# A hybrid attention and convolution layer: the convolution of tiles 1 to 4 in two column blocks ahead of attention, output weights loaded behind the last k projection, four output tiles beside the last attention chunks

## The chip, the cores and the metric

The kernel runs on one core of a Trainium2 chip. The metric is the time of one execution on the device in microseconds (us); what is compared is the median of several runs. A profiled execution is one more run, recorded by the hardware; its rows give the busy time of each engine: PE (TensorE), DVE (VectorE), ACT (ScalarE), POOL (GpSimd) and SP, whose queue issues the DMA transfers. "PEld" is TensorE's weight load. The "clock" of a stretch is the TensorE clock granted in it, where 1.00 is 2.4 GHz and 0.50 is 1.2 GHz.

## What is computed

One layer over 2048 prompt frames and 8 x 16 sample frames, all in float32, model width 1024 (17 tiles of 128 frames: tile 0 holds the sample frames, tiles 1 to 16 the prompt):

```python
def layer(x, p_i, k_cache, v_cache, conv_cache, prm, i):
    hn = rmsnorm(x, prm['norm_mix'][i])
    proj = hn @ prm['w_in'][i]
    q, k, v, a, g = jnp.split(proj, SPLITS, axis=-1)
    ...
    attn = swa_prompt(q, k, v, sinks)          # or swa_sample for the sample frames
    ...
    u = a * jax.nn.sigmoid(g)
    c, new_conv = depthwise_causal(u, prm['conv_w'][i], prm['conv_b'][i], conv_cache)
    c = jax.nn.silu(layernorm(c, prm['ln_g'][i], prm['ln_b'][i]))
    merged = jnp.concatenate([rmsnorm(attn, prm['attn_out_g'][i]), rmsnorm(c, prm['conv_out_g'][i])], axis=-1)
    x = x + merged @ prm['w_out'][i]
    hf = rmsnorm(x, prm['norm_ffn'][i])
    x = x + jnp.square(jax.nn.relu(hf @ prm['w_up'][i])) @ prm['w_down'][i]
    gate = jax.nn.sigmoid(rmsnorm(x, prm['norm_ple'][i]) @ prm['w_ple_gate'][i])
    x = x + (p_i @ prm['w_ple'][i]) * gate
```

Attention runs in chunks of 64 frames over a window of 128 earlier frames (8 query heads, 2 key heads, width 64, with sinks). The convolution is depthwise over 512 channels with 31 taps.

## The kernel before

**Arithmetic.** Every large product is made of float32 operands split into a high and a low part, so that one product is three matmuls (high by high, high by low, low by high). `weight()` brings one row block of a weight in: a load into `raw` (three buffers), a cast on ACT into the high half of `w` and a subtraction on POOL (or DVE) for the low half. `wpool` has eight `w` buffers.

**Stages.** They follow each other on TensorE.
- **A** (L286 to L328): six blocks of up to three tiles. Norm, transposition and split into `hn`, which is stored to `H` in memory, then the projections a and g and their product into `U0` to `U3` (prompt, 512 frames each) and `US` (sample).
- **B** (L457 to L525): eight blocks of two tiles (the first has tile 0 too). Each loads its part of `H` back into eight `hnb` buffers, computes the projections k, v and then the four of q from six weight blocks `wq`, and runs four chunks of attention: scores `s`, a softmax on DVE and ACT (`pr`), transpositions `pt`, copies `p`, the product with v (`o`), copies into `mta`, a store to `M[t]`. One sample batch goes with each block.
- **C** (L536 to L585): for a tile, load `M[t]` and `x`, split `M[t]`, 48 matmuls with the eight weight blocks `wo` of `w_out`, residual, `X1[t]` stored, and the sum of its squares for the next norm. One tile (tile 1, `EARLY`) stands inside stage B's pools; the other eight follow.
- **MLP** (L690 to L745): five blocks of up to four tiles, 4096 hidden columns in eight groups, weights streamed. Tiles 9 to 16 have their output projection (`c_late`) between the groups of blocks 0 and 1. Then the gated embedding.

**The convolution** is cut into steps (`conv_steps`): in each, column blocks 0 to 2 are done by DVE, three multiply-adds into PSUM (L207), and column block 3 (`PCB`) by ACT, which scales a `tap`, and POOL, which adds it (L199, L200). A block of tiles takes 31 steps and one more for each tile (`conv_post`: norm, activation, transposition, store to `M[t]`). The generator `conv_a` goes through tile 0, tiles 1 to 4 and tiles 5 to 8; `A_STEPS` says how many steps follow each of a block's four column blocks in stage A, `B_STEPS` how many follow each chunk in B. Of the 102 steps of `conv_a` A takes 52 and B 50. Tiles 9 to 16 are stepped in the MLP.

**The order of the work.** A scheduler lays out one in-order queue for each engine from priorities that follow the program's text; `later` shifts the priority of what it wraps (by `BEHIND` for convolution steps, by `-PREO` for `load_wo`, by `-PRE` for `wq`), and `issue_after` keeps what it wraps behind a given instruction on that instruction's queue. Inside a queue nothing overtakes.

Of the kernel before, what the change touches and what calls it, by code (L numbers as in the profile page):

```python
# [39 lines left out]
CONV_A = [[0], [1, 2, 3, 4], [5, 6, 7, 8]]  # L40
A_STEPS = {1: 4, 2: 4, 3: 2, 4: 2, 5: 1}
B_STEPS = (2, 2)
CONV_LATE = {0: [9, 10, 11, 12], 1: [13, 14, 15, 16]}
# [8 lines left out]
EARLY = 1  # L52
# [5 lines left out]
PCB = (3,)  # L58
# [17 lines left out]
def build(ctx, tc, nc, a):  # L76
# [97 lines left out]
    def conv_steps(tiles):  # L174
# [15 lines left out]
        own = [(cb, j) for cb in range(4) if cb not in PCB for j in range(KC)]  # L190
        per = len(own) // KC
        for j in range(KC):
            for cb in PCB:
# [29 lines left out]
    conv_a = (x for tiles in CONV_A for x in conv_steps(tiles))  # L223
# [233 lines left out]
    for bi, tiles in enumerate(B_BLOCKS):  # L457
# [156 lines left out]
    def c_late_half(t, h, xt, ms):  # L614
# [8 lines left out]
        for nh in range(2):  # L623
            xs = xt[:, nh * 512:(nh + 1) * 512]
            nc.vector.scalar_tensor_tensor(xs, pd[nh], ors[:, t, h:h + 1], xs, ALU.mult, ALU.add)

    def c_late(tiles):

        load_wo()
        for i in range(0, len(tiles), 2):  # L630
            pair = [(t, *c_late_front(t)) for t in tiles[i:i + 2]]
            for h in range(2):
                for t, xt, ms in pair:
                    c_late_half(t, h, xt, ms)
            for t, xt, ms in pair:
                nc.sync.dma_start(X1[t], xt)
                ss = fpool.tile([P, 2], F32, name="osl", bufs=2)
                for nh in range(2):
                    sq = fpool.tile([P, 512], F32, name="sqx", tag="relu", bufs=2)
                    nc.scalar.activation(sq, xt[:, nh * 512:(nh + 1) * 512], AF.Square, accum_out=ss[:, nh:nh + 1])  # L640
                nc.gpsimd.tensor_tensor(ss[:, 0:1], ss[:, 0:1], ss[:, 1:2], ALU.add)
# [225 lines left out]
```

## Time and profile before

| | |
|---|---|
| median of three runs | 2563.26 us (2559.66 to 2565.75) |
| profiled execution | 2565.52 us, span 2563.7 us |
| mean granted TensorE clock | 0.986 |
| busy, share of the span | PE 98%, DVE 44%, ACT 41%, POOL 42% |

The span goes from the first to the last instruction; 1.8 us of the execution lie outside it. A busy share is an average over stages: PE is full through the MLP and gives way only at a few places, and what those places wait for has to be read one by one. A matmul's end is modelled, so that a PE that is busy at a clock of 0.50 does half of what it would at 1.00.

### The profile page before, as it was taken

The page shows a single profiled execution, that of the slowest core. Times are in us where ns is not written, and L with a number is a line of the kernel's source. Part 1 is how long each engine was busy: PE and PEld are TensorE (multiplying, and loading weights), DVE is VectorE, ACT ScalarE, POOL GpSimd, SP SyncE. Part 2 cuts the span into 40 slices and gives each one's busy share as a digit, 9 for nine tenths or more (in the row PEclk, how much of TensorE's full clock was granted, in tenths as well). Part 3 has the DMA queues.
Part 4 walks back from the last instruction along what each step waited for, and adds up shares of the span by engine and source line. Part 5 has one row for each costly group of instructions (what it writes and reads, how often), then busy time and mean ns, then how long its engine had stood idle before and what let it go on. Part 6 is the DMA issues. An engine that isn't in the chain of part 4 may idle for free.

```text
span 2563.7 us, 32974 instructions
## 1 busy us (share of the span) xinstructions
PE 2503.8 (98%) x12575; PEld 2120.4 (83%) x12575; DVE 1115.8 (44%) x1874; ACT 1060.9 (41%) x2027; POOL 1084.7 (42%) x783
## 2 busy tenths in 40 slices
PE   8998999997999999999999999999999999999998
PEld 8998877665888888888888888888899998998887
DVE  3654647663355543455535242222322234344433
ACT  6362467675232223633233332323233334454343
POOL 5062034036264444855343543435355555642222
PEclk9998999997999999999999999999999999999999
DMA  8434222222452232523234552323344336553221
GB/s 242 152 121 147 78 96 71 83 81 91 155 197 100 95 111 90 206 83 115 83 115 148 184 199 81 115 74 120 120 163 132 131 124 208 186 189 115 91 72 49
DMA packets 121998, 321.39 MB, mean 125 GB/s; under 512 B 15728, under 2 KB 49264, under 8 KB 121840
## 3 DMA queue, kind: packets, MB, share of 16 engines
q1 hardware_dynamic: 121840, 319.29, 37.1%
q8 instruction: 98, 1.61, 0.3%
q14 instruction: 60, 0.49, 0.1%
HBM read 264.95 MB, written 54.29 MB: 125 GB/s over the span
## 4 chain that ended last, share of the span: by engine, by line
PE 94%; ACT 2%; DMA 2%; DVE 1%; POOL 1%; issue 1%; SPq 0%; POOLq 0%; ACTq 0%; DVEq 0%
PE up L273 29%; PE d L729 29%; PE mm L273 12%; PE pg L751 7%; PE acc L546 4%; PE accl L620 3%; PE o L404 2%; PE pq L758 2%; PE s L376 1%; DMA hnb<-H 1%; PE pt L398 1%; PE tr L661 1%; PE tr L261 1%; PE pt L392 0%; PE up L261 0%
## 5 line engine op out<-in xcount | busy, mean ns | idle before, releaser
L121 POOL TENSOR_TENSOR w<-raw,w 128x1024 fp32r<-128x1024 f32 x305 | 731.5, 2412 | 708.5 <-ACT w L120 707.2
L273 PE MATMUL up<-hf,w 128*128 128x512 f32 (+2 forms) x3840 | 761.5, 357 | 0.5 <-DVE ht L715 0.5
L729 PE MATMUL d<-w,ht 128*128 128x512 f32 x3264 | 759.7, 390 | 0.3 <-ACT ht L713 0.3
L273 PEld LDWEIGHTS up<-hf,w 128*128 128x128 f32 x3840 | 659.4, 189 | 93.2 <-DVE ht L715 1.3
L729 PEld LDWEIGHTS d<-w,ht 128*128 128x128 f32 x3264 | 609.8, 188 | 125.7 <-ACT ht L713 0.8
L120 ACT CAST w<-raw 128x1024 fp32r<-128x1024 f32 x330 | 345.9, 1050 | 651.0 <-PE d L729 457.2
L735 DVE TENSOR_TENSOR accf<-d,accf 128x512 f32<-128x512 f32 x272 | 176.1, 686 | 386.7 <-PE d L729 386.1
L207 DVE SCALAR_TENSOR_TENSOR c<-U,vec,c 128x512 f32<-128x512 f32 x348 | 261.3, 751 | 6.1
L714 DVE SCALAR_TENSOR_TENSOR up<-up,relu 128x512 f32<-128x512 f32 (+2 forms) x160 | 98.9, 618 | 311.9 <-ACT relu L712 311.7
L273 PE MATMUL mm<-hn,w 128*128 128x384 f32 (+1 forms) x1152 | 200.1, 331 | 0.9 <-ACT hn L263 0.8
L273 PE MATMUL mm<-hnb,w 128*128 128x256 f32 (+1 forms) x1152 | 180.8, 307 | 15.2 <-DMA hnb<-H 11.9
L273 PEld LDWEIGHTS mm<-hn,w 128*128 128x128 f32 x1152 | 190.5, 190 | 1.7 <-ACT hn L263 1.7
L200 POOL TENSOR_TENSOR acc<-acc,tap 128x512 f32<-128x512 f32 (+1 forms) x150 | 169.3, 1129 | 44.5 <-ACT tap L199 33.9
L712 ACT ACTIVATE relu<-up 128x512 f32<-128x512 f32 (+2 forms) x160 | 84.9, 531 | 244.5 <-PE up L273 244.0
L273 PEld LDWEIGHTS mm<-hnb,w 128*128 128x128 f32 x1152 | 158.1, 196 | 32.6 <-issue 23.7
L715 DVE TENSOR_TENSOR ht<-up,ht 128x512 fp32r<-128x512 f32 (+2 forms) x160 | 97.7, 611 | 109.8 <-ACT ht L713 105.8
L751 PE MATMUL pg<-w,xg 128*128 128x512 f32 x510 | 125.2, 392 | 0.0
L751 PEld LDWEIGHTS pg<-w,xg 128*128 128x128 f32 x510 | 94.7, 188 | 18.8
L199 ACT ACTIVATE tap<-U,vec 128x512 f32<-128x512 f32 x120 | 85.0, 722 | 30.6 <-POOL acc L200 29.8
L454 POOL TENSOR_TENSOR ors<-ors,mhalf 128x1 f32<-128x1 f32 x17 | 10.5, 616 | 196.3 <-DVE ors L453 196.2
L546 PE MATMUL acc<-w,ms 128*128 128x512 f32 x384 | 91.3, 397 | 1.2 <-ACT ms L120 1.2
L713 ACT ACTIVATE ht<-relu 128x512 fp32r<-128x512 f32 (+2 forms) x160 | 90.6, 566 | 1.3
(182 smaller groups left out, 2203.1 us busy)
## 6 DMA issues: line engine op xcount, KB each, us to landing
raw<-in_w_up SPq DMA_DIRECT2D x160, 512.0 KB, 3.5
raw<-in_w_down SPq DMA_DIRECT2D x160, 512.0 KB, 3.5
H<-hn SPq DMA_DIRECT2D x20, 768.0 KB, 4.9
hnb<-H SPq DMA_DIRECT2D x56, 256.0 KB, 4.2
xt<-in_x SPq DMA_DIRECT2D x17, 512.0 KB, 6.1
xnf<-X SPq DMA_DIRECT2D x17, 512.0 KB, 5.7
accf<-X SPq DMA_DIRECT2D x17, 512.0 KB, 5.1
X<-accf SPq DMA_DIRECT2D x17, 512.0 KB, 3.2
```

The lines of the kernel that those rows point to most:

```text
L120: nc.scalar.copy(hi, src)
L121: (eng or nc.gpsimd).tensor_tensor(lo, src, hi.bitcast(F32), ALU.subtract)
L200: nc.gpsimd.tensor_tensor(acc, acc, t, ALU.add)
L207: nc.vector.scalar_tensor_tensor(accs[cb] if i == KC - 1 else pacc, view(cb, i), w_, pacc, ALU.mult, ALU.add)
L273: nc.tensor.matmul(ps, w(wp, k), m[:, ap_, 0:n], start=(i == 0), stop=(i == 3 * KD - 1))
L546: nc.tensor.matmul(ps, ms[:, ap_, k, :], wo[k][:, wp, nh * 512:(nh + 1) * 512], start=(i == 0), stop=(i == 11))
L713: nc.scalar.activation(ht[:, 0, 0:n], r[:, 0:n], AF.Square)
L714: nc.vector.scalar_tensor_tensor(ps[:, 0:n], ps[:, 0:n], 0.0, r[:, 0:n], ALU.max, ALU.mult)
L715: hs = nc.vector.tensor_tensor(ht[:, 1, 0:n], ps[:, 0:n], ht[:, 0, 0:n].bitcast(F32), ALU.subtract)
L729: nc.tensor.matmul(pd[nh], hts[f][:, hp, i * P:(i + 1) * P], wds[f][:, wp, nh * 512:(nh + 1) * 512], start=(j == 0), stop=(j == 3 * GRP - 1))
L735: ad = nc.vector.tensor_tensor(xs, pd[nh], xs, ALU.add)
L751: nc.tensor.matmul(pg, xg[ap_][:, k * P:(k + 1) * P], wg[k][:, wp, ns], start=(i == 0), stop=(i == 3 * KD - 1))
```

## The change

- `conv_steps` takes the column blocks of ACT and POOL for each block of tiles: tiles 1 to 4 give them blocks 2 and 3, and DVE two multiply-adds a step in place of three. The other blocks of tiles stay.
- `A_STEPS` puts 64 steps into A in place of 52, `B_STEPS` 38 into B in place of 50: the 31 steps of tiles 1 to 4 now all stand in A.
- Tiles 1 to 4 (`EARLY`) have their output projection inside stage B's pools, on buffers that are done there: the split in quarters of 256 columns in `hnb`'s eight buffers, `M[t]` in `US`'s, x and sum in `U0`'s and `U1`'s.
- In stage C and there the split of `M[t]` goes in four quarters, and the sum of squares on ACT is taken of each half, into the PSUM tile, and added on POOL. `c_late` does the same.
- `load_wo` is wrapped in `issue_after` with the last block's k projection.
- The convolution of tiles 9 to 16 is one generator over both MLP blocks.

```diff
-CONV_A = [[0], [1, 2, 3, 4], [5, 6, 7, 8]]
-A_STEPS = {1: 4, 2: 4, 3: 2, 4: 2, 5: 1}
-B_STEPS = (2, 2)
-CONV_LATE = {0: [9, 10, 11, 12], 1: [13, 14, 15, 16]}
+CONV_A = [([0], (3,)), ([1, 2, 3, 4], (2, 3)), ([5, 6, 7, 8], (3,))]
+CONV_LATE = [([9, 10, 11, 12], (3,)), ([13, 14, 15, 16], (3,))]
+A_STEPS = {1: 4, 2: 4, 3: 3, 4: 3, 5: 2}
+B_STEPS = (1, 2)
...
-EARLY = 1
+EARLY = 4
...
-PCB = (3,)
...
-    def conv_steps(tiles):
+    def conv_steps(tiles, pcb):
...
-    with later(tc, -PREO):
+    with later(tc, -PREO), tc.issue_after(kproj.ins):
         load_wo()
 
-    def c_tile(t, pl, ps_, mt, xt, ms, acct):
+    def residual(t, nh, xt, acc, h, ss):
+
+        xs = xt[:, nh * 512:(nh + 1) * 512]
+        nc.vector.scalar_tensor_tensor(xs, acc, ors[:, t, h:h + 1], xs, ALU.mult, ALU.add)
+        if h:
+            nc.scalar.activation(acc, xs, AF.Square, accum_out=ss[:, nh:nh + 1])
+
+    def c_end(t, xt, ss):
+        nc.sync.dma_start(X1[t], xt)
+        nc.gpsimd.tensor_tensor(ss[:, 0:1], ss[:, 0:1], ss[:, 1:2], ALU.add)
+        rstd(rs1[:, t:t + 1], ss[:, 0:1], 1.0 / D)
+
+    def c_tile(t, ps_, mt, xt, ms, acct):
+
         nc.sync.dma_start(mt, M[t])
         nc.sync.dma_start(xt, a["x"][t])
-        split(ms[:, 0], ms[:, 1], mt)
+        for i, m in enumerate(ms):
+            split(m[:, 0], m[:, 1], mt[:, 2 * i:2 * i + 2])
+        ss = cpool.tile([P, 2], F32, name="oss")
...
-                xs = xt[:, nh * 512:(nh + 1) * 512]
-                nc.vector.scalar_tensor_tensor(xs, ps, ors[:, t, h:h + 1], xs, ALU.mult, ALU.add)
-        nc.sync.dma_start(X1[t], xt)
-        ss = pl.tile([P, 1], F32, name="oss", bufs=2)
-        nc.scalar.activation(mt.rearrange("p k n -> p (k n)"), xt, AF.Square, accum_out=ss)
-        rstd(rs1[:, t:t + 1], ss, 1.0 / D)
-
-    for t in F_BLOCKS[0][:EARLY]:
-        mx_ = upool.tile([P, 2, D], F32, name="mxe", tag="U1", bufs=1)
-        c_tile(t, bpool, psb, mx_[:, 0].rearrange("p (k n) -> p k n", k=8), mx_[:, 1],
-               upool.tile([P, 2, 8, P], F32R, name="mse", tag="U0", bufs=1),
+                residual(t, nh, xt, ps, h, ss)
+        c_end(t, xt, ss)
+
+    xe = [upool.tile([P, 2, D], F32, name="xe", tag=f"U{i}", bufs=1) for i in range(2)]
+    for i, t in enumerate(F_BLOCKS[0][:EARLY]):
+        c_tile(t, psb, upool.tile([P, 8, P], F32, name="mte", tag="US", bufs=1), xe[i // 2][:, i % 2],
+               [bpool.tile([P, 2, 2, P], F32R, name="mse", tag="hnb", bufs=8, align_bytes=ALN) for _ in range(4)],
                dict(tag="mm"))
```

Lines of the changed kernel stand one lower than before from `conv_steps` on (L199 for L200), a few higher from the k projection on, and L564 for L546.

**SP's queue between A and B.** The last stores of `hn`, the last loads of `w_in` for `wq`, loads of `w_out`, and the first block's loads of `H`. Before:

```order
L294 DMA H<-hn 128x4x256 x4
L128 DMA raw<-in_w_in 128x1024 x3
L128 DMA raw<-in_w_out 128x1024 x4
L462 DMA hnb<-H 128x2x384 x8
L416 DMA vc<-in_cache_vt 128x128
L418 DMA ks<-in_cache_kt 128x128
L416 DMA vc<-in_cache_vt 128x128
L418 DMA ks<-in_cache_kt 128x128
L513 DMA out_new_conv_prompt<-U_141 512x1x30
L128 DMA raw<-in_w_out 128x1024
```

Now:

```order
L295 DMA H<-hn 128x4x256 x4
L127 DMA raw<-in_w_in 128x1024 x3
L127 DMA raw<-in_w_out 128x1024
L463 DMA hnb<-H 128x2x384 x8
L417 DMA vc<-in_cache_vt 128x128
L419 DMA ks<-in_cache_kt 128x128
L417 DMA vc<-in_cache_vt 128x128
L419 DMA ks<-in_cache_kt 128x128
L516 DMA out_new_conv_prompt<-U_141 512x1x30
L127 DMA raw<-in_w_out 128x1024 x4
```

Of the four loads of `w_out` that stood ahead of the first block's `hnb` one still does. The other three moved behind these loads, with a fifth that stood there before. None of the five moved to the last block's k projection: `load_wo` has no instruction on TensorE's queue, which is the one that `issue_after` orders here. The last three loads of `w_out` stand behind the last block's `hnb`, before and now.

**POOL's queue between A and B.** `w` by L121 (now L120) is the low half of a `wq` block; `acc` by L200 (L199) is a tap of the convolution. Before:

```order
L200 TENSOR_TENSOR acc_1454<-acc_1454,tap_3089 128x512
L200 TENSOR_TENSOR acc_1454<-acc_1454,tap_3095 128x512
L200 TENSOR_TENSOR acc_1454<-acc_1454,tap_3147 128x512
L326 COPY U3_141<-U2_140 128x4x30
L121 TENSOR_TENSOR w_2328<-raw_2326,w_2328 128x1024
L121 TENSOR_TENSOR w_2333<-raw_2331,w_2333 128x1024
L121 TENSOR_TENSOR w_2338<-raw_2336,w_2338 128x1024
L121 TENSOR_TENSOR w_2343<-raw_2341,w_2343 128x1024
L121 TENSOR_TENSOR w_2348<-raw_2346,w_2348 128x1024
L121 TENSOR_TENSOR w_2353<-raw_2351,w_2353 128x1024
L456 MEMSET qb_2318 128x1024
```

Now:

```order
L199 TENSOR_TENSOR acc_1453<-acc_1453,tap_2095 128x512
L199 TENSOR_TENSOR acc_1454<-acc_1454,tap_2098 128x512
L120 TENSOR_TENSOR w_2483<-raw_2481,w_2483 128x1024
L120 TENSOR_TENSOR w_2488<-raw_2486,w_2488 128x1024
L120 TENSOR_TENSOR w_2493<-raw_2491,w_2493 128x1024
L199 TENSOR_TENSOR acc_1453<-acc_1453,tap_2223 128x512
L199 TENSOR_TENSOR acc_1454<-acc_1454,tap_2226 128x512
L120 TENSOR_TENSOR w_2498<-raw_2496,w_2498 128x1024
L120 TENSOR_TENSOR w_2503<-raw_2501,w_2503 128x1024
L199 TENSOR_TENSOR acc_1453<-acc_1453,tap_2231 128x512
L199 TENSOR_TENSOR acc_1454<-acc_1454,tap_2234 128x512
L120 TENSOR_TENSOR w_2508<-raw_2506,w_2508 128x1024
```

Ahead of the fourth of the six `wq` blocks 48 taps of tiles 1 to 4 stand now, in two chains (`acc_1453` and `acc_1454`), where 30 stood; two stand between the third and the fourth, two between the fifth and the sixth, and ten follow.

**TensorE's queue at the end of B.** `o` is the product with v of one chunk, `s` scores, `pr` a softmax's result that is transposed into `pt`. Before (L546, one output tile, ends some 20 such lines further up, behind the last q projection):

```order
L152 MATMUL c<-ident,acc 128x128 x4
L435 MATMUL o<-vc,p_5805 128x128
L436 MATMUL o<-vn,p_5805 128x128
L440 MATMUL pt<-ident,on 128x128
L376 MATMUL s<-kt,qt 128x192 x4
L452 MATMUL pt<-ones,sra 128x1
L392 MATMUL pt<-ident,pr 128x128 x4
L398 MATMUL pt<-ident,pr 64x128 x4
L404 MATMUL o<-p_5859,va 128x512
L392 MATMUL pt<-ident,pr 128x128 x4
L169 MATMUL c<-ident,z 128x128 x4
L404 MATMUL o<-p_5866,va 128x512
```

Now (L564 is the output projection of tiles 1 to 4):

```order
L168 MATMUL c<-ident,z 128x128 x4
L377 MATMUL s<-kt,qt 128x192 x2
L441 MATMUL pt<-ident,on 128x128
L377 MATMUL s<-kt,qt 128x192 x2
L564 MATMUL acc<-w,mse 128x512 x24
L453 MATMUL pt<-ones,sra 128x1
L393 MATMUL pt<-ident,pr 128x128 x4
L564 MATMUL acc<-w,mse 128x512 x12
L399 MATMUL pt<-ident,pr 64x128 x4
L405 MATMUL o<-p_5918,va 128x512
L393 MATMUL pt<-ident,pr 128x128 x4
L405 MATMUL o<-p_5925,va 128x512
```

The 192 matmuls of four tiles stand between the last q projection and the last row shown with L564, spread among attention of the seventh block's chunks and parts of `conv_post`. Behind it six chunks follow up to stage C with nothing between them, as before. Stage C then has five tiles in place of eight.

**ACT's queue at the end of B,** up to the first split of stage C. Before:

```order
L199 ACTIVATE tap<-U_140,vec 128x512 x2
L394 COPY p_6347<-pt 128x512
L199 ACTIVATE tap<-U_140,vec 128x512
L408 COPY mta<-o 64x4x64 x2
L199 ACTIVATE tap<-U_140,vec 128x512
L199 ACTIVATE tap<-U_141,vec 128x512
L408 COPY mta<-o 64x4x64 x2
L199 ACTIVATE tap<-U_141,vec 128x512
L448 ACTIVATE pt<-mta 128x512
L448 ACTIVATE pt<-mts 128x512
L120 CAST ms<-mt 128x1024 x2
```

Now:

```order
L443 COPY mts<-pt 64x4x16 x2
L198 ACTIVATE tap<-U_141,vec 128x512 x2
L386 ACTIVATE pr<-pr,rc 128x192
L395 COPY p_6360<-pt 128x512
L395 COPY p_6406<-pt 128x512
L409 COPY mta<-o 64x4x64 x4
L449 ACTIVATE pt<-mta 128x512
L449 ACTIVATE pt<-mts 128x512
L119 CAST ms<-mt 128x256 x8
```

From the copy that stands for the product `o<-p_5866` (now `p_5925`) to the first split `ms`, 27 taps of tiles 9 to 12 and 13 to 16 stood in ACT's queue and 18 stand now.

## Rows read from the trace of the kernel before

**Rows 1.** The page: busy time of PE, and the chain that ended last by engine.

```profile
PE 2503.8 (98%) x12575; PEld 2120.4 (83%) x12575; DVE 1115.8 (44%) x1874; ACT 1060.9 (41%) x2027; POOL 1084.7 (42%) x783
...
PE 94%; ACT 2%; DMA 2%; DVE 1%; POOL 1%; issue 1%; SPq 0%; POOLq 0%; ACTq 0%; DVEq 0%
```

**Rows 2.** Busy time by stretch: PE, PEld, DVE, ACT, POOL, PE's clock, DMA share, GB/s.

```profile
205.00:232.00 27.00, 17.17 (x140) 17.00 (x140) 18.74 (x27) 9.60 (x12) 15.12 (x7) 0.84 0.64 212
260.00:532.00 272.00, 259.42 (x1641) 202.93 (x1639) 172.09 (x395) 180.95 (x594) 54.91 (x61) 0.98 0.26 83
384.00:391.00 7.00, 6.70 (x29) 6.25 (x30) 6.63 (x15) 6.99 (x24) 4.56 (x4) 0.52 0.14 49
416.00:421.00 5.00, 4.14 (x20) 3.51 (x20) 3.28 (x7) 3.87 (x12) 4.60 (x5) 0.70 0.00 0
531.90:564.80 32.90, 29.37 (x143) 19.89 (x141) 19.55 (x45) 21.53 (x72) 9.79 (x19) 1.00 0.23 81
564.80:619.70 54.90, 39.82 (x127) 21.00 (x126) 21.08 (x55) 43.44 (x113) 42.56 (x41) 0.66 0.13 44
619.70:712.40 92.70, 92.70 (x417) 76.50 (x418) 36.11 (x47) 23.29 (x32) 27.95 (x24) 0.98 0.47 165
712.40:2311.00 1598.60, 1597.74 (x7670) 1360.50 (x7669) 636.51 (x935) 573.03 (x803) 790.55 (x406) 1.00 0.40 135
```

**Rows 3.** What PE waited for, 200 to 625 us: total, times, longest.

```profile
PE mm L273 <- DMA hnb<-H: 11.9, 4, 9.8
```

**Rows 4.** The chain that ended last, 195 to 245 us: start, length, what.

```profile
215.40 2.43 POOL w L121
...
217.84 3.52 DMA raw<-in_w_out
...
224.32 6.91 DMA hnb<-H
...
231.36 10.73 PE mm L273 x45
```

**Rows 5.** SP's queue, 205 to 232 us: start, length, what.

```profile
217.84 6.43 SPq L128 DMA_DIRECT2D raw<-in_w_out  x4
```

**Rows 6.** POOL from 143 to 245 us: start, length, what, [idle before <- releaser].

```profile
183.08 6.82 POOL L200 TENSOR_TENSOR acc<-acc,tap 128x512 f32<-128x512 f32 x5 [0.40 <-ACT tap L199]
198.34 0.29 POOL L326 COPY U<-U 128x120 f32<-128x120 f32 x1 [8.44 <-DVE U L320]
208.31 14.23 POOL L121 TENSOR_TENSOR w<-raw,w 128x1024 fp32r<-128x1024 f32 x6 [9.68 <-ACT w L120]
```

**Rows 7.** DVE's convolution in 260 to 532 us: busy, mean ns | idle before.

```profile
L207 DVE SCALAR_TENSOR_TENSOR c<-U,vec,c 128x512 f32<-128x512 f32 x117 | 87.5, 748 | 0.9
...
L207 DVE SCALAR_TENSOR_TENSOR acc<-U,vec,c 128x512 f32<-128x512 f32 x5 | 3.7, 743 | 0.0
```

**Rows 8.** PE from 519 to 568 us: start, length, what, [idle before <- releaser].

```profile
543.53 4.13 PE L546 MATMUL acc<-w,mse 128*128 128x512 f32 x17
...
561.84 0.33 PE L440 MATMUL pt<-ident,on 128*128 128x128 f32 x1 [1.59 <-DVE on L438]
...
567.05 1.06 PE L398 MATMUL pt<-ident,pr 128*64 128x128 f32 x4 [0.69 <-DVE ors L453]
```

**Rows 9.** Taps in 564.8 to 619.7 us: busy, mean ns | idle before, releasers.

```profile
L200 POOL TENSOR_TENSOR acc<-acc,tap 128x512 f32<-128x512 f32 x28 | 35.4, 1264 | 3.9 <-ACT tap L199 2.6
L199 ACT ACTIVATE tap<-U,vec 128x512 f32<-128x512 f32 x30 | 21.0, 720 | 3.7 <-POOL acc L200 3.2
```

**Rows 10.** The chain that ended last, 560 to 680 us.

```profile
579.39 1.27 POOL acc L200
...
618.56 1.05 ACT ms L120
...
644.34 10.95 PE acc L546 x48
```

**Rows 11.** POOL's first split of stage C.

```profile
619.68 2.38 POOL L121 TENSOR_TENSOR ms<-mt,ms 128x1024 fp32r<-128x1024 f32 x1 [0.35 <-ACT ms L120]
```

More of the change, by code (lines that the diff above doesn't have):

```diff
@@ L188, in view @@
             return U[c0 // 512][:, cb, c0 % 512 + j:c0 % 512 + j + n]
-        own = [(cb, j) for cb in range(4) if cb not in PCB for j in range(KC)]
+        own = [(cb, j) for cb in range(4) if cb not in pcb for j in range(KC)]
         per = len(own) // KC
         for j in range(KC):
-            for cb in PCB:
+            for cb in pcb:
                 w_, acc = cw[:, j, cb:cb + 1], accs[cb]
@@ L221, in steps @@
                 next(gen, None)
-    conv_a = (x for tiles in CONV_A for x in conv_steps(tiles))
+    conv_a = (x for block in CONV_A for x in conv_steps(*block))
+    conv_l = (x for block in CONV_LATE for x in conv_steps(*block))
     pa = ExitStack()
@@ L272, in proj @@
             for wp, ap_ in ((0, 0), (0, 1), (1, 0)):
-                nc.tensor.matmul(ps, w(wp, k), m[:, ap_, 0:n], start=(i == 0), stop=(i == 3 * KD - 1))
+                mm = nc.tensor.matmul(ps, w(wp, k), m[:, ap_, 0:n], start=(i == 0), stop=(i == 3 * KD - 1))
                 i += 1
+        return mm
     for t in A_BLOCKS[0]:
@@ L474, in build @@
             ps = psb.tile([P, 512], F32, name="mm")
-            proj(ps[:, 0:n], lambda wp, k: wq[i][:, wp, k * P:(k + 1) * P], lambda k: hns[k], n)
+            pj = proj(ps[:, 0:n], lambda wp, k: wq[i][:, wp, k * P:(k + 1) * P], lambda k: hns[k], n)
             src = ps[:, o:n]
+            if i == 4:
+                kproj = pj
             if i < 4:
@@ L584, in build @@
     for t in (F_BLOCKS[0] + F_BLOCKS[1])[EARLY:] + [0]:
-        c_tile(t, opool, ps2, opool.tile([P, 8, P], F32, name="mt"), opool.tile([P, D], F32, name="xc"),
-               opool.tile([P, 2, 8, P], F32R, name="ms", align_bytes=ALN), dict(bufs=4))
+        c_tile(t, ps2, opool.tile([P, 8, P], F32, name="mt"), opool.tile([P, D], F32, name="xc"),
+               [opool.tile([P, 2, 2, P], F32R, name="ms", bufs=8, align_bytes=ALN) for _ in range(4)], dict(bufs=4))
         if t == F_BLOCKS[1][-2]:
@@ L623, in c_late_half @@
         for nh in range(2):
[L624 to L625 removed]
+            residual(t, nh, xt, pd[nh], h, ss)
     def c_late(tiles):
@@ L630, in c_late @@
         for i in range(0, len(tiles), 2):
-            pair = [(t, *c_late_front(t)) for t in tiles[i:i + 2]]
+            pair = [(t, *c_late_front(t), fpool.tile([P, 2], F32, name="osl", bufs=3)) for t in tiles[i:i + 2]]
             for h in range(2):
[L633 to L641, printed above, removed]
-                rstd(rs1[:, t:t + 1], ss[:, 0:1], 1.0 / D)
+                for t, xt, ms, ss in pair:
+                    c_late_half(t, h, xt, ms, ss)
+            for t, xt, ms, ss in pair:
+                c_end(t, xt, ss)
     def ple_front(t):
@@ L696, in build @@
             accs.append(acc)
-        late = conv_steps(CONV_LATE[bi]) if bi in CONV_LATE else iter(())
         for g in range(NFF // GRP):
@@ L716, in build @@
                 if f % 2:
-                    steps(late, 1, hs)
+                    steps(conv_l, 1, hs)
             if last:
@@ L735, in build @@
                     ad = nc.vector.tensor_tensor(xs, pd[nh], xs, ALU.add)
-                steps(late, 1, ad)
+                steps(conv_l, 1, ad)
         for i, t in enumerate(tiles):
```

4 lines of the change are left out of this document (2 added, 2 removed).

## The prediction, made before the changed kernel ran

> **What bounds the kernel now.** The page first: PE is busy 2503.8 of 2563.7 us, and the chain that ended last runs over PE for 94% [rows 1]. So a change helps only where PE stands idle or runs at half clock. The stretches show where that is: through the MLP, 712.4 to 2311 us, PE is busy 1597.74 of 1598.60 us at clock 1.00 [rows 2], and nothing there can give time back. What is left is ahead of 712 us, at three places.
>
> At the border of A and B PE stands still 9.8 us of 27 [rows 2]: the longest wait of PE is for `hnb`, 9.8 us [rows 3]. The chain says why: the fourth low half of `wq` on POOL ends at 217.84, only then a `raw` buffer is free for the load of `w_out`, the last of four such loads holds SP's queue 6.43 us, and `hnb` is issued at 224.32 and lands 6.91 us later [rows 4, 5].
>
> In B, 260 to 532 us, PE is idle 272.00 - 259.42 = 12.6 us, and its clock falls at two places: 0.52 in 384 to 391, where DVE is busy 6.63 of 7 us and ACT 6.99, and 0.70 in 416 to 421 [rows 2]. Half clock costs 7 x 0.48 + 5 x 0.30 = 4.9 us there.
>
> At B's end, from 531.9 on, one output tile fills PE until 547.66 [rows 8]; PE is idle 3.5 us up to 564.8, with waits of 1.59 and 0.69 us on DVE behind the filler [rows 2, 8]. Then, up to 619.7, six chunks run without any: PE is busy 39.82 of 54.90 us at clock 0.66, ACT 43.44, POOL 42.56 [rows 2]. Stage C is full again, 92.70 of 92.70 [rows 2], at 10.95 us for a tile's 48 matmuls [rows 10].
>
> **The sum** is made against the profiled execution, 2565.5 us, and then moved by 2.3 us to the median of 2563.3.
>
> *1. Border of A and B.* The change takes three loads of `w_out` out of SP's queue ahead of `hnb`, up to 6.43 us [rows 5]. But it puts 18 more taps and one more first product ahead of the fourth split. At the 6.82 / 5 = 1.364 us that a tap takes on POOL at the end of A, plus 0.8, that is 25.3 us; POOL was idle 8.44 + 9.68 = 18.1 us there [rows 6]. The split ends some 7.2 us later, at 225.0; the one load left goes out, and `hnb` behind it at about 225.4, against 224.32. What SP saves, POOL gives away: 0. The bounds: -6 if the taps find more idle time ahead of 183 us and only SP's 6.43 counts, +5 if the load still takes 3.52 us [rows 4] and its split on ACT and DVE before SP goes on. The last split, ahead of the last q projection, has the two taps between in its way, 2.7 us, and PE's 10.73 us of the k projection [rows 4] cover it.
>
> The Trainium skill (GPSIMD Engine Reference, section 4.1, Engine selection) sends an elementwise operation of two inputs to VectorE, since GpSimd takes about twice as long; it speaks against moving a column block from DVE to POOL. The rows agree in direction, 1.26 to 1.36 us against 0.75, a factor of 1.7 to 1.8 [rows 6, 7, 9]. By the page's factor, an estimate, a tap would take 1.5 us and the 18 taps another 2.4 us of the border.
>
> *2. Stage B.* Of 122 multiply-adds of DVE in 260 to 532 us [rows 7] tiles 5 to 8 need 3 x 31 = 93; the other 29 go, 29 x 0.75 = 21.8 us of DVE's 172.09 [rows 2, 7]. ACT keeps its 180.95 [rows 2], and about twelve taps come into the first chunks. At stake are 12.6 + 4.9 = 17.5 us. DVE and ACT are both full where the clock falls, and DVE alone loses an eighth, so I take a bit under a third: -5, between 0 (ACT alone limits) and -10 (PE's waits fall with DVE's and the clock stays up).
>
> *3. The four tiles.* Three tiles more, 144 matmuls, move from C into B's end. In C they cost 3 x 10.95 = 32.9 us, all of which goes there. In B's end they cost the same, less what they fill: the 3.5 us idle in 531.9 to 564.8, and about 1.5 us (0.69 of it idle, the rest clock) up to the matching row at 567.05 [rows 2, 8]. I take -4, since the filler reaches up to the last row ahead of the six chunks; bounds -5 and +3. The +3 stands for new waits: `mse` has `hnb`'s buffers, which are free only as the last q projection reads them out, so ACT's first cast can't start earlier, and what is queued on ACT and POOL behind the 16 quarter splits is the softmax of the same chunks, for which PE waits next. A quarter of the 1.05 us cast and the 2.38 us split [rows 10, 11] is 0.9 us a quarter; PE holds another tile's 10.95 us meanwhile. The load of the next `M[t]` waits for the four splits of the one ahead (one buffer); load and splits must stay under 10.95 us.
>
> *4. The six chunks.* They keep their content and still have no filler. ACT has 9 taps fewer (27 down to 18 in the queue), POOL 9 additions fewer: 9 x 0.72 = 6.5 us of ACT and 9 x 1.26 = 11.4 us of POOL [rows 9], of 43.44 and 42.56 busy in 54.9 us [rows 2]. Some of these taps are on the chain itself (POOL at 579.39 [rows 10]). The chain alternates over four engines, so only part of it comes back: -5, with bounds of +2 (the taps were in gaps) and -15 (all of POOL's, and the clock longer at 1.00).
>
> *5. C's start* waits for a cast of 1.05 us and the split of 2.38 us [rows 10, 11]; in quarters the first is 0.9 us in all: -1.5, bounds 0 and -2.5. Five tiles of C then run as eight did. Square in two halves on ACT has as many columns as before, and one small addition on POOL.
>
> *6. The MLP:* 0. The output tiles' PSUM there is freed by ACT instead of DVE, hidden by the other tile's half, 24 matmuls or 5.5 us by [rows 10]; were that cover gone, it would be a few tenths for each of 8 tiles.
>
> Sum: 0 - 5 - 4 - 5 - 1.5 = -15.5. That is 2550.0 profiled and, 2.3 lower, **2548** for the median.
>
> **The rivals.** *(a) The clock holds.* If the filler leaves softmax so far ahead that PE never idles long in the six chunks, the loss is not 5 but all that the clock takes there, 54.9 x (1 - 0.66) = 18.7 us [rows 2]: 2548 - 13.7 = 2534. For it: the half clock begins behind the waits of [rows 8]. Against: PE's own work at full clock would be 39.82 x 0.66 = 26 us in 54.9, so the chunks are bound by their chain. The rule beside it is in the Trainium skill (TensorE: Matmul & The Clock Gate, Terms): the penalty is the throttled time times the share of pulses withheld. By it all 18.7 us could come back; the trace bears it out only where PE itself is the wait.
>
> *(b) Work is moved and nothing filled.* The four tiles stand in an in-order queue, the chunks around them wait for DVE and ACT as before, DVE's relief in B goes to gaps (ACT full), the loads of `w_out` aren't held to the last block, contrary to the change's words, and only term 5 is left: 2562, no change. For it: PE was 100% busy while the old tile filled it, and the idle time behind is small [rows 2].
>
> *(c) Slower: POOL late at the border.* Everything behind the fourth split hangs on it, one us for one us: `raw`, SP, `hnb`, PE. It decides for slower than 2568.4 when the split comes 20 us later than I said, at 245 us, which is when the 48 taps take 0.42 us more each, 1.78 us: two chains whose taps wait on ACT. At 24 us, 2572. Against it: POOL waited 0.40 us for a tap in the row with five [rows 6].
>
> **From this to the numbers.** The forecast has 0.50 (its own range 2541 to 2556), (a) 0.17, (b) 0.21, (c) 0.12. A measurement tells 0.2%, 5.1 us, from no change, so faster is under 2558.1. The forecast and (a) are faster but for the forecast's upper edge, 0.03; a third of (b) falls there too, since DVE's relief alone makes it 2557; the rest of (b) is the same, and 0.01 of (c). Faster 0.71, same 0.18, slower 0.11. The range is 2531 to 2565: below it stands a third of (a), 0.06, above it (c), 0.11.
>
> **What would show it.** Right: PE's wait for `hnb` stays about 9 to 11 us, with the fourth split on POOL at 222 to 228; PE's idle time in B is some 5 us less; PE full from the last q projection to the last of 192 matmuls; the six chunks take 46 to 50 us up to C's first matmul against 52.6 from 567.05, with the clock at half again; five C tiles in about 55 us. Wrong: waits of PE for `mse` or `w` in the four tiles, ACT waiting for `M[t]` ahead of a softmax, `hnb` past 230 us, the clock at 1.00 in the six chunks, or idle time in the MLP, which by the sum has none.

## The result and the profile after

The changed kernel takes 2549.1 us (median of four runs, 2544.6 to 2550.1) where the kernel before takes 2563.8 (median of four beside them): a ratio of 0.9936, 95% interval 0.9921 to 0.9951, 16 us or 0.6% faster by the ratio (the medians differ by 14.7). The profiled execution has a span of 2547.5 us where it had 2563.7, at a mean clock of 0.991.

The page of the changed kernel, busy times and the chain by engine:

```profile
PE 2495.1 (98%) x12575; PEld 2116.7 (83%) x12575; DVE 1103.5 (43%) x1843; ACT 1088.4 (43%) x2102; POOL 1128.7 (44%) x850
...
PE 94%; DMA 2%; ACT 2%; issue 1%; POOL 1%; DVE 1%; SPq 0%; POOLq 0%; ACTq 0%; DVEq 0%
```

As before [rows 1] the chain lies on PE. PE is busy 8.7 us less with the same 12575 matmuls: they did not become fewer, and the mean clock rose from 0.986 to 0.991.

Stretches of the changed kernel (columns as in [rows 2]):

```profile
205.00:232.00 27.00, 22.05 (x157) 21.44 (x156) 18.01 (x25) 14.42 (x21) 27.00 (x17) 0.90 0.56 198
260.00:532.00 272.00, 262.80 (x1660) 205.81 (x1661) 153.99 (x365) 188.41 (x617) 59.27 (x70) 0.98 0.27 90
260.00:360.00 100.00, 99.11 (x689) 82.42 (x690) 60.26 (x139) 77.71 (x243) 46.59 (x50) 1.00 0.30 99
360.00:412.00 52.00, 48.26 (x296) 36.99 (x295) 27.00 (x67) 28.68 (x102) 1.65 (x3) 0.97 0.18 60
518.00:586.02 68.02, 68.02 (x317) 50.21 (x317) 36.14 (x72) 45.35 (x131) 37.47 (x56) 1.00 0.23 85
586.02:634.96 48.94, 32.57 (x117) 16.84 (x115) 18.13 (x47) 34.24 (x98) 28.52 (x29) 0.80 0.13 46
634.96:695.40 60.44, 60.44 (x273) 49.96 (x273) 24.57 (x32) 20.59 (x48) 20.87 (x34) 0.96 0.45 168
695.40:2295.00 1599.60, 1598.08 (x7674) 1361.77 (x7673) 644.39 (x939) 574.81 (x804) 792.10 (x407) 1.00 0.39 135
```

and of the kernel before, two parts of stage B:

```profile
260.00:360.00 100.00, 97.78 (x660) 79.52 (x657) 53.23 (x135) 56.63 (x205) 6.08 (x15) 1.00 0.27 87
360.00:412.00 52.00, 49.92 (x295) 39.17 (x294) 39.90 (x79) 42.83 (x125) 34.95 (x32) 0.93 0.24 78
```

What PE waited for in the changed kernel, 200 to 640 us:

```profile
PE pt L453 <- DVE sra L451: 7.5, 4, 2.9
...
PE mm L273 <- DMA hnb<-H: 3.6, 4, 2.4
PE pt L453 <- ACT tap L198: 2.6, 1, 2.6
PE c L151 <- DVE acc L206: 2.4, 1, 2.4
```

Two kinds of landmark stand in every trace: the square of the attention's result of a tile on ACT (`pt<-mta`), and the first product `o` of the first of the last six chunks. With them the difference splits into pieces, the 32.85 us of three tiles' matmuls (3 x 10.95 [rows 10]) taken off where four are early:

| stretch | before, us | after, us | difference |
|---|---|---|---|
| start to tile 1's square | 291.17 | 286.74 | -4.4 |
| to tile 11's square | 224.25 | 219.92 | -4.3 |
| to the first `o` of the last six chunks | 52.48 | 79.79 - 32.85 | -5.5 |
| to C's first matmul | 51.76 | 48.51 | -3.3 |
| to the end | 1944.04 | 1912.54 + 32.85 | +1.3 |

The table is of one trace each, and such pieces vary: the change and experiments 4 and 5, which have the same edits up to tile 1's square, have it at 284.6 to 287.9 us, and the last piece spreads over 1.4 us among kernels with one early tile. So a microsecond or two in one row shows little by itself.

Of the rows: PE's longest wait for `hnb` went from 9.8 to 2.4 us [rows 3], but just ahead of it PE now waits 2.4 us for DVE's last product of the convolution (`acc`); PE is full for the whole of the four tiles, 68.02 of 68.02 us; the six chunks have 48.94 us at clock 0.80 where they had 54.90 at 0.66 from a little earlier on [rows 2]; C and the MLP are as full as they were, and took 1.3 us more, 0.8 of it in C.

### The profile page after: what moved, and what is told of

The parts are those of the page before. It is cut to its first block, busy times and chain, and to the rows that moved or that the text cites. A ratio compares the mean times of both kernels' runs of the same rounds, so it can differ in the third digit from the quotient of the medians.

```text
span 2547.5 us, 33055 instructions
## 1 busy us (share of the span) xinstructions
PE 2495.1 (98%) x12575; PEld 2116.7 (83%) x12575; DVE 1103.5 (43%) x1843; ACT 1088.4 (43%) x2102; POOL 1128.7 (44%) x850
## 4 chain that ended last, share of the span: by engine, by line
PE 94%; DMA 2%; ACT 2%; issue 1%; POOL 1%; DVE 1%; SPq 0%; POOLq 0%; ACTq 0%; DVEq 0%
PE d L735 29%; PE up L273 29%; PE mm L273 12%; PE pg L757 7%; PE acc L564 4%; PE accl L634 3%; PE o L405 2%; PE pq L764 2%; PE s L377 1%; DMA hnb<-H 1%; PE pt L399 1%; PE pt L393 1%; PE tr L668 1%; PE tr L261 1%; POOL w L120 0%
## 5 line engine op out<-in xcount | busy, mean ns | idle before, releaser
L120 POOL TENSOR_TENSOR w<-raw,w 128x1024 fp32r<-128x1024 f32 x305 | 730.5, 2411 | 677.9 <-ACT w L119 675.1
L206 DVE SCALAR_TENSOR_TENSOR c<-U,vec,c 128x512 f32<-128x512 f32 x319 | 239.6, 751 | 5.9
L199 POOL TENSOR_TENSOR acc<-acc,tap 128x512 f32<-128x512 f32 (+1 forms) x180 | 207.4, 1162 | 42.8 <-ACT tap L198 33.8
L198 ACT ACTIVATE tap<-U,vec 128x512 f32<-128x512 f32 x150 | 106.8, 722 | 43.9 <-POOL acc L199 43.1
L634 PE MATMUL accl<-w,msl 128*128 128x512 f32 x384 | 87.2, 389 | 0.0
L634 PEld LDWEIGHTS accl<-w,msl 128*128 128x128 f32 x384 | 72.1, 188 | 14.9
```

The costliest lines, as they stand in the source:

```text
L120: (eng or nc.gpsimd).tensor_tensor(lo, src, hi.bitcast(F32), ALU.subtract)
L198: nc.scalar.activation(t, view(cb, j), AF.Copy, scale=w_)
L199: nc.gpsimd.tensor_tensor(acc, acc, t, ALU.add)
L206: nc.vector.scalar_tensor_tensor(accs[cb] if i == KC - 1 else pacc, view(cb, i), w_, pacc, ALU.mult, ALU.add)
L634: nc.tensor.matmul(pd[nh], ms[h][:, ap_, k, :], wo[4 * h + k][:, wp, nh * 512:(nh + 1) * 512], start=(i == 0), stop=(i == 11))
```

## The experiments

All were timed against the kernel before; differences are (1 - ratio) x 2564 us.

**1. The convolution's part alone**, on the kernel before:

```diff
-CONV_A = [[0], [1, 2, 3, 4], [5, 6, 7, 8]]
-A_STEPS = {1: 4, 2: 4, 3: 2, 4: 2, 5: 1}
-B_STEPS = (2, 2)
+CONV_A = [([0], (3,)), ([1, 2, 3, 4], (2, 3)), ([5, 6, 7, 8], (3,))]
+A_STEPS = {1: 4, 2: 4, 3: 3, 4: 3, 5: 2}
+B_STEPS = (1, 2)
```

> The kernel before with the convolution's part of the change alone (second column block of tiles 1 to 4 on ACT and POOL, the new A and B steps); one early output tile, splits and squares as before. My theory, that the gains are separate and add: the border of A and B comes 4 us sooner and stage B another 4, the end of B and the six chunks stay within 2 us: 8 to 10 us faster, 2554 to 2556. Rival, that the whole gain hangs on the four tiles as filler: at most 2 us faster, 2562 or more.

Measured: 0.9945 (0.9933 to 0.9957), 14 us faster, span 2547.4: within the uncertainty the whole gain of the change. The border is that of the changed kernel (tile 1's square at 286.27). On SP's queue one load of `w_out` stands ahead of `hnb` here too, without `issue_after`; in experiment 2, with `issue_after` and the old tables, four do, as before. Experiment 1 and then 2:

```profile
220.94 0.33 SPq L127 DMA_DIRECT2D raw<-in_w_out  x1
```

```profile
216.93 6.53 SPq L127 DMA_DIRECT2D raw<-in_w_out  x4
```

So the convolution's part moved the three loads, and the wrapped `load_wo` did not; that it did so through POOL's later splits is argued, not shown. I had expected less, because I gave it nothing in the last six chunks; they take 48.70 us here with as many taps beside them as before, 27:

```profile
555.72:604.42 48.70, 32.94 (x117) 16.92 (x116) 18.14 (x50) 41.81 (x109) 40.97 (x39) 0.75 0.14 50
```

and in the changed kernel, with 18:

```profile
586.45:634.96 48.51, 32.14 (x114) 16.41 (x112) 17.90 (x47) 33.95 (x97) 28.09 (x29) 0.80 0.13 46
```

**2. The four tiles without the convolution's part:** the changed kernel with the three tables above as they were, one column block on POOL.

> The changed kernel with the convolution's steps and columns of before; the four early tiles, quartered splits and squares stay. My theory: the border and B go as in the kernel before, the four tiles take their 32.9 us less 5, the six chunks 0 to 4 us less: 5 to 8 us faster than before, 2556 to 2559. Rival, that the tiles only fill because the convolution is out of the way: 0 to 2 us faster; second rival, that they do it all: 13 or more, 2551.

Measured: 0.9972 (0.9962 to 0.9982), 7 us faster, as expected. With 1, the two parts alone come to 21 us and together to 16; the uncertainty of that difference is about as large as the difference. Its six chunks take 48.69 us, with 18 taps:

```profile
596.04:644.73 48.69, 34.36 (x113) 17.41 (x111) 16.92 (x47) 33.89 (x97) 28.09 (x29) 0.72 0.14 48
```

Each part alone, and both together, bring the chunks to 48.5 to 48.7 us. In the four tiles' stretch (tile 11's square to the first `o`, three tiles' matmuls taken off) this run has 46.92 us, the convolution's part alone 50.59, the change 46.94, the kernel before 52.48. These are the two pieces in which the parts don't add.

**3. The loads of `w_out` behind `hnb`**, on the kernel before, and nothing else:

```diff
-            nc.sync.dma_start(h[:, :, 0:n].bitcast(F32), H[:, k, :, ...])
+            hd = nc.sync.dma_start(h[:, :, 0:n].bitcast(F32), H[:, k, :, ...])
+            hd0 = hd if bi == 0 else hd0
...
-    with later(tc, -PREO):
+    with later(tc, -PREO), tc.issue_after(hd0.ins):
```

> The kernel before, with the loads of w_out held behind the first block's loads of hnb on SP's queue and nothing else. My theory, that SP's queue alone makes the border: hnb is issued at about 218 us in place of 224.3 and PE starts B 4 to 6 us sooner, all of it kept to the end: 2558 to 2560. Rival, that the border's gain comes from elsewhere (transfers land no sooner, or the lost clock was cheap): 0 to 1 us, 2563.

Measured: 0.9953 (0.9941 to 0.9965), 12 us faster, twice what I had expected. SP's queue and the chain of this run:

```profile
211.02 5.06 SPq L128 DMA_DIRECT2D raw<-in_w_in  x3
216.14 5.03 SPq L462 DMA_DIRECT2D hnb<-H  x8
```

```profile
203.59 26.05 PE mm L273 x197
```

`hnb` is issued 8.2 us sooner than before [rows 4], behind the loads of `w_in` and without a wait for POOL's fourth split, and PE goes from A into B without a pause. Tile 1's square, before and here:

```profile
291.17 0.61 ACT L448 ACTIVATE pt<-mta 128x512 f32<-128x512 f32 x1
```

```profile
277.90 0.60 ACT L448 ACTIVATE pt<-mta 128x512 f32<-128x512 f32 x1
```

That is 13.3 us sooner for a wait of 9.8 (experiment 2, with SP's order of before, has the square at 289.14, so some 2 us of this can be the trace's). PE's first matmuls behind the wait, before and here:

```profile
231.36 11.24 PE L273 MATMUL mm<-hnb,w 128*128 128x384 f32 x48 [9.83 <-DMA hnb<-H]
```

```profile
221.65 8.50 PE L273 MATMUL mm<-hnb,w 128*128 128x384 f32 x48
```

The same 48 matmuls take 2.7 us less. In 232 to 240 us the clock was 0.68 before, so partly at the lower level, with PE busy for all 8 us; it is 1.00 here. Taking the wait away gave 2.7 us more than the wait by these rows.

**4. No taps beside the last chunks:** the changed kernel, the convolution of tiles 9 to 16 held in the MLP on ACT as well:

```diff
-                nc.scalar.activation(r[:, 0:n], ps[:, 0:n], AF.Relu)
+                rl = nc.scalar.activation(r[:, 0:n], ps[:, 0:n], AF.Relu)
...
-                    steps(conv_l, 1, hs)
+                    steps(conv_l, 1, hs, rl)
...
-                steps(conv_l, 1, ad)
+                steps(conv_l, 1, ad, rl)
```

> The changed kernel with the convolution of tiles 9 to 16 held back into the MLP on ACT too, so that no tap stands beside the last six chunks (19 on ACT do in the changed kernel, 30 before). My theory, that the taps stretch the chunks' chain: if 9 taps fewer brought 3 to 4 us, all 19 bring 4 to 8 more, six chunks in 41 to 45 us in place of 49, 2541 to 2545. Rival, that taps lie in gaps and the chain is DVE, ACT and PE in turn: within 1.5 us of the changed kernel, 2548 to 2550. The MLP has slack on ACT and POOL and should not show it.

Measured: 0.9888 (0.9875 to 0.9901), 29 us faster than before and 12 faster than the changed kernel. The same stretch as above, from the first `o` to stage C:

```profile
584.15:622.67 38.52, 28.93 (x112) 14.54 (x110) 15.72 (x47) 22.91 (x79) 6.30 (x11) 0.87 0.16 60
```

38.52 us in place of 48.51. POOL's busy time fell from 28.09 to 6.30 us, ACT's from 33.95 to 22.91. The taps in the changed kernel's stretch, and what they waited for:

```profile
L199 POOL TENSOR_TENSOR acc<-acc,tap 128x512 f32<-128x512 f32 x18 | 22.8, 1265 | 1.7 <-ACT tap L198 0.6
...
L198 ACT ACTIVATE tap<-U,vec 128x512 f32<-128x512 f32 x18 | 12.8, 720 | 2.8 <-POOL acc L199 2.7
```

ACT takes a tap only when POOL has added an earlier one (two `tap` buffers), and while it waits, 2.7 us in all, the exponentials and copies behind it in ACT's queue wait too. The wait of PE on a tap, 2.6 us in the rows of waits above, is gone. Of the 10.0 us in the chunks 6.8 are idle time of PE (16.4 to 9.6 us) and 3.2 its busy time. The spans differ by 14.5 us; the rest lies ahead of the chunks (2.3) and behind them (2.2).

**5. Tiles 3 and 4 held among the last chunks:** each group of 12 matmuls behind the `o` of a given chunk.

```diff
+                    st.enter_context(tc.issue_after(OM[hold[2 * nh + h]].ins))
...
-               dict(tag="mm"))
+               dict(tag="mm"), {2: (26, 26, 27, 27), 3: (28, 28, 29, 30)}.get(i, ()))
```

> The changed kernel with the output projections of tiles 3 and 4 held among the last chunks: each group of 12 matmuls stands on TensorE's queue behind the product with v of chunk 26, 26, 27, 27 (tile 3) and 28, 28, 29, 30 (tile 4). My theory, that filler is worth what PE idles beside it: in the six chunks PE idles 16 of 49 us and half of the rest is at half clock, in the stretch ahead it was full with four tiles; 5 to 10 us faster than the changed kernel, 2539 to 2544. Rival, that the chunks are delayed by as much as the filler takes: 0 to 2 us, 2547 to 2549.

Measured: 0.9912 (0.9898 to 0.9926), 6 us faster than the changed kernel by the ratios. The intervals touch, so a gain is likely and its size open.

**6 and 7. Both orders, with four early tiles and with one:** experiment 4 with the two edits of 3; then `EARLY = 1` in it.

> The changed kernel with no taps of tiles 9 to 16 beside the last chunks, and the loads of w_out held behind the first block's hnb on SP's queue. My theory: the one load of w_out that still stands ahead of hnb waits for POOL's fourth split, so hnb is issued at about 217 us in place of 222 and the two gains add: 4 to 6 us faster than without taps alone, 2530 to 2533. Rival, that POOL's taps at the border hold the last splits of wq and PE waits there instead: 0 to 1 us, 2536.

> The same with one early output tile in place of four, so with three tiles more in stage C. My theory, that the tiles gain nothing where they stand once the convolution is out of the way (the convolution's part alone was as fast as the whole change): within 2 us of the run with four. Rival, that they fill 4 to 5 us of waits behind the last q projection: 4 to 5 us slower.

Measured: 0.9859 (0.9846 to 0.9872) with four, 0.9902 (0.9888 to 0.9916) with one. The first adds 7 us to experiment 4, a little more than expected. The second refutes me: without taps the three tiles are worth 11 us, in the profile 9.2. With one tile, tile 11's square to the first `o`, and from there to C:

```profile
495.62:550.11 54.49, 51.13 (x266) 37.37 (x267) 31.71 (x80) 37.98 (x122) 13.59 (x28) 0.94 0.18 66
550.11:593.81 43.70, 33.04 (x116) 16.96 (x116) 14.90 (x46) 22.93 (x79) 6.11 (x10) 0.77 0.14 48
```

With four the first stretch is full, and the second takes 40.32:

```profile
496.40:575.58 79.18, 79.18 (x415) 61.09 (x416) 41.67 (x91) 46.47 (x146) 24.75 (x47) 1.00 0.26 95
575.58:615.90 40.32, 30.20 (x113) 14.96 (x111) 15.81 (x47) 22.95 (x79) 6.33 (x11) 0.85 0.17 58
```

So of the tiles' gain 54.49 - (79.18 - 32.85) = 8.2 us lies in the stretch that they fill, and 3.4 in the chunks behind; other pieces give some 2 us of it back.

**8 and 11. Both orders, and the tiles held,** first as in 5, then up to the last chunk: tile 3 behind 26, 27, 28, 28, tile 4 behind 29, 30, 31, 31.

> No taps beside the last chunks, w_out behind hnb, and tiles 3 and 4 held among chunks 26 to 30. My theory: PE idles 9.6 of the 32.7 us that the six chunks take without taps and loses 5 more to the clock; the held tiles fill 6 to 10 of it: 2521 to 2526, the fastest of all. Rival, that without taps the chain is so short that filler only delays it: 2530 or more.

> No taps beside the last chunks, w_out behind hnb, tiles 3 and 4 held among the last chunks up to the last: tile 3 behind chunks 26, 27, 28, 28, tile 4 behind 29, 30, 31, 31, so that two groups of 12 matmuls stand in the gap ahead of stage C. My theory: they fill the 5.5 us in which PE waits there for the last statistics and the load of M, and C starts at full clock: 2522 to 2526, 4 to 7 faster than with the tiles held earlier. Rival, that C's first load starts only when the last group is done, as its buffers come free then: 2529 or more.

Measured: 0.9863 (0.9848 to 0.9877) and 0.9867 (0.9853 to 0.9882): no difference from 6. The spans were 2524.5 and 2531.4 us against 2527.9. In 11 the rival happened; the chain ahead of C:

```profile
608.11 5.67 PE acc L568 x24
...
613.80 0.75 DVE xe L543
...
615.00 5.04 DMA mt<-M
...
620.12 0.41 ACT ms L119
```

The last group's residual ends at 614.55, and only then is C's first `M[t]` loaded, 5.04 us, with PE idle for 4.92 of C's wait. That filler doesn't help a shortened chain in 8 is measured; why is not shown.

**9. The two orders alone**, on the kernel before: 3 and 4 with none of the change.

> The kernel before with two orders alone and none of the change: the loads of w_out behind the first block's hnb, and the convolution of tiles 9 to 16 held back into the MLP. My theory, that the border (11 us by the run with w_out alone) and the taps beside the last chunks (12 us from the changed kernel to the one without taps) add here too: 2540 to 2544, faster than the whole change. Rival, that taps cost so much only behind four tiles: 2549 to 2554.

Measured: 0.9910 (0.9895 to 0.9926), 23 us faster: 11 more than 3 alone, from which it differs in the taps only. The six chunks of experiment 3, with 30 taps, and of this run, with none:

```profile
555.73:608.74 53.01, 37.32 (x117) 18.65 (x116) 20.36 (x51) 43.09 (x110) 44.22 (x42) 0.69 0.13 46
```

```profile
558.25:600.79 42.54, 31.75 (x117) 15.99 (x116) 17.52 (x51) 24.70 (x80) 6.99 (x12) 0.82 0.16 55
```

Two edits of the order of work do no less than the change.

**10. Without the second column block:** experiment 6 with the convolution's tables of before.

> Four early tiles, w_out behind hnb, no taps beside the last chunks, and the convolution's steps and columns of before. It takes POOL's second column block away from the border. My theory: the border is 3 us sooner than with it (278 against 281 us at the first tile's statistics), B gives 4 us back to DVE and ACT: 2529 to 2532, so that the second column block is worth 0 to 2 us once SP's queue is right. Rival, that it is worth what its part of the change brought, 14 us: 2540 or more.

Measured: 0.9878 (0.9862 to 0.9895), 5 us slower than 6 by the ratios, but the intervals overlap; the spans, 2530.9 and 2527.9, say 3. It is not the 14 us that the part brought alone, and my 0 to 2 is not refuted. Tile 1's square comes 3.0 us sooner here than in 6 (278.11 for 281.09), and from it to tile 11's square the run takes 6.8 us longer (222.10 for 215.31): the part costs at the border and pays in B.

**12. The changed kernel with `w_out` behind `hnb`:**

> The changed kernel with the loads of w_out held behind the first block's hnb and nothing else. My theory: hnb is issued at 216 in place of 222 us and all of it comes back, 5 to 7 us, 2542 to 2544. Rival, that POOL's taps in the first block eat it: 2547 to 2549.

Measured: 0.9904 (0.9890 to 0.9919), 8 us faster than the change. Tile 1's square in the changed kernel, in this one, and in experiment 10, which has the convolution's tables of before:

```profile
286.74 0.64 ACT L449 ACTIVATE pt<-mta 128x512 f32<-128x512 f32 x1
```

```profile
280.65 0.63 ACT L449 ACTIVATE pt<-mta 128x512 f32<-128x512 f32 x1
```

```profile
278.11 0.60 ACT L449 ACTIVATE pt<-mta 128x512 f32<-128x512 f32 x1
```

These price the border. Of the 13.3 us that SP's order alone gives, the change got 4.4; 6.1 (4 to 7 by the traces of experiments 4 and 5) hang on the one load of `w_out` that it left ahead of `hnb`, and 2.5 to 2.8 on the convolution's part (the square comes at 280.3 to 281.5 us in the five runs with it and with `w_out` behind `hnb`, and at 277.9 to 278.7 in the three without it). PE at the border here, and in experiment 10:

```profile
223.74 0.44 PE L151 MATMUL c<-ident,acc 128*128 128x128 f32 x2 [2.51 <-DVE acc L206]
223.93 10.16 PE L273 MATMUL mm<-hnb,w 128*128 128x384 f32 x48
```

```profile
221.40 8.50 PE L273 MATMUL mm<-hnb,w 128*128 128x384 f32 x48
```

It is not POOL for which PE waits there. With all steps of tiles 1 to 4 in A, the first transposition of their finished convolution stands on PE's queue ahead of the k projection, and waits 2.5 us for DVE's last product.

## Why the prediction was right, and where it wasn't

The forecast was 2548 and the kernel takes 2549.1; the likeliest case came. Its sum, -15.5, is the -16.2 of the two profiled spans to within a microsecond. That is in part luck: two terms gave more than I said, by 4.4 and 1.5 us, and two less, by 1.7 and 1.5, with 0.7 less in B and 1.3 lost behind C's start.

*Term 1, the border,* was 0 and is -4.4. The steps were right in kind: the fourth split moved, and SP followed it. POOL and SP of the changed kernel:

```profile
181.84 16.39 POOL L199 TENSOR_TENSOR acc<-acc,tap 128x512 f32<-128x512 f32 x13 [0.65 <-ACT tap L198]
...
209.70 7.12 POOL L120 TENSOR_TENSOR w<-raw,w 128x1024 fp32r<-128x1024 f32 x3
216.78 2.54 POOL L199 TENSOR_TENSOR acc<-acc,tap 128x512 f32<-128x512 f32 x2
219.29 4.72 POOL L120 TENSOR_TENSOR w<-raw,w 128x1024 fp32r<-128x1024 f32 x2
```

```profile
221.73 0.33 SPq L127 DMA_DIRECT2D raw<-in_w_out  x1
222.11 4.98 SPq L463 DMA_DIRECT2D hnb<-H  x8
```

The fourth split is the first of the two from 219.29 on and ends 4.72 / 2 = 2.4 us behind it, at 221.7, where I had 225.0: the taps took 16.39 / 13 = 1.26 us, not 1.364. The load of `w_out` goes out then and `hnb` 0.4 us later, 2.2 us sooner than before. PE there, to be read against the kernel before's row in experiment 3:

```profile
224.55 0.44 PE L151 MATMUL c<-ident,acc 128*128 128x128 f32 x2 [2.38 <-DVE acc L206]
227.35 11.37 PE L273 MATMUL mm<-hnb,w 128*128 128x384 f32 x48 [2.36 <-DMA hnb<-H]
240.50 0.44 PE L507 MATMUL pt<-ident,vt 128*128 128x128 f32 x2 [1.78 <-ACT vt L487]
```

The k and v projections start 4.0 us sooner: 2.2 by the issue, and 1.8 because they start 5.2 us behind it where it was 7.0. So the mis-sized step is the split's time, with a landing that I took as it was. The lower clock behind the wait is no part of it: these matmuls take 11.37 us where they took 11.24. Some 2 us of the 4.0 are lost again, in the wait for ACT's copy of `vt`, and the rest of the -4.4 lies in the first block's attention, which no experiment took apart. My sign, a wait of 9 to 11 us for `hnb`, failed: it is 2.4, beside a new one of 2.4 for DVE. The bound of -6 for SP's side was too near: SP's order alone gives -13.3 (experiment 3), and there the clock does count.

*Term 2, stage B,* was -5 and is -4.3, but not as I had it. I said that ACT keeps its time there. Over 260 to 532 us it does (188.41 against 180.95 [rows 2]); around the place where the clock fell it doesn't: in 360 to 412 ACT fell from 42.83 to 28.68 us and POOL from 34.95 to 1.65, DVE from 39.90 to 27.00. The taps of tiles 5 to 8 run sooner, in 260 to 360, where ACT went from 56.63 to 77.71. That cost 3.4 us from tile 2's square to tile 4's (51.5 us before, 54.9 after), brought 9.3 from there to tile 6's (49.1 before, 39.8 after), and tiles 8 to 11 gave 2.4 back (61.6 before, 64.0 after). That the tables do this is shown by experiments 10 and 6, which differ in them alone: the first stretch is 3.0 us longer with the part, the second 8.9 shorter.

*Term 3, the four tiles,* was -4 and is -5.5 on the changed kernel's path. PE is full through them, and none of the waits that I feared (`mse`, `M[t]`, `w_out`) is in the rows. Alone the tiles bring 5.6 us there (experiment 2), the convolution's part alone 1.9 (experiment 1), and both together 5.5: on top of that part the tiles' share is 3.6.

*Term 4, the six chunks,* was -5 and is -3.3, and whether by its reason, nine taps fewer, is open. With the old tables four tiles and nine taps fewer bring 3.1 us (51.76 to 48.69, experiment 2); with the new ones they bring 0.2 (48.70 to 48.51), since the convolution's part had already brought 3.1 with all 27 taps. Taking out all taps, and nothing else, shortens the chunks by 10.5 us where 30 stand (experiments 3 and 9), and by 10.0 and 8.3 where 18 stand (the change and 4, 12 and 6). So the price is not one for each tap, as I had it by its share of ACT's and POOL's busy time; but these kernels differ in more than taps, and with one tile and the new tables all 27 make only 5.0 (1 and 7, which differ in other edits too). Why the convolution's part shortens the chunks with the taps still there stays open; its clock is 0.75 there, against 0.66:

```profile
567.90:619.66 51.76, 37.39 (x117) 19.21 (x116) 17.98 (x48) 40.36 (x107) 39.78 (x38) 0.66 0.14 47
```

*Term 5, C's start,* was -1.5 and is 0. PE waits 1.14 us for the first split where it waited 1.15: what ends last there is the high half on ACT and the load of `M[t]`, and POOL's half, the longest that I shortened, had been running beside the first matmuls already [rows 11]. Behind it 1.3 us were lost, no more than this piece varies between like kernels.

*Rival (a),* the clock held, did not happen in the change (0.80), and experiment 4 shows its mistake: the chunks lost 10 us when taps went, the clock rose from 0.80 to 0.87 only, and 6.8 of the 10 were idle time of PE. Where PE is the wait, the clock's price comes back: 2.7 us at the border in experiment 3. The rule that I set beside the rival (the Trainium skill, TensorE: Matmul & The Clock Gate, Terms) gives as an estimate 8 x (1 - 0.68) = 2.6 us for 232 to 240 us, and the trace agrees there, with the 2.7 us.

*Rival (b)* was right on one point, that `issue_after` does nothing here, and wrong on the gain.

*Rival (c):* POOL was late, 221.7 against 217.8 us, but not by the 20 us that this rival needs. A tap took 1.26 us on POOL against 0.75 for a multiply-add on DVE, a factor of 1.7. The Trainium skill (GPSIMD Engine Reference, section 4.1, Engine selection) puts an operation of two inputs at about twice VectorE's time; the rows agree in direction. Even so the convolution's part, which moves a column block to POOL, gave the larger gain of the two parts, and what it costs at the border, 2.5 to 2.8 us, is a wait for DVE.

What is shown: SP's order alone is worth 12 us at the border, of which the change gets a third; the convolution's part alone brings the whole gain within the uncertainty; the taps beside the last chunks cost 11 to 12 us in each of three pairs of runs that differ in them alone (3 and 9, 12 and 6, the change and 4). The tiles fill their stretch in every run with four, but what that is worth depends on the rest: 7 us with the old tables (2), 0 to 2 on top of the convolution's part (1 against the change), 11 when the taps are gone (7 against 6). That the taps hide the tiles' gain in the change is argued from the last two. What stays open: why either part alone shortens the chunks as much as both, and what makes up the border's -4.4 behind the k and v projections.

## What to carry to other kernels

A wait of the engine that bounds the kernel is dearer than its length when a lower clock follows it (here by 2.7 us on 9.8): look at the clock behind the wait before pricing it. Before filling ahead of a latency-bound stretch, clear the queues of its chain's engines of work that isn't due: here that gave 11 to 12 us each time, and the filler brought more behind it (11 us) than without it (0 to 2). And see in the queues what a wrapped order does: here the loads moved with the convolution's tables, and the call that was to move them moved nothing.

## What the runs showed that I had not expected

The two edits of order gave 23 us on the kernel before, and the change 16. The 18 taps that the change leaves beside the last chunks cost nearly as much there (8.3 and 10.0 us) as 30 do in the kernel before with `w_out` behind `hnb` (10.5). The fastest kernels are 6 and 8, 2529.5 and 2529.4 us, 36 and 35 us faster than the kernel before.
